# Queueing one engine's share of a second chain behind the first at the seam of two blocks

## The chip, the cores and the metric

The kernel runs on one core of a Trainium2 chip. The core has a matmul engine (TensorE, PE in the rows, with its weight loads as PEld), two vector engines with different abilities (VectorE, DVE; GpSimd, POOL), an activation engine (ScalarE, ACT) and a queue that issues the transfers from memory (SyncE, SP). Each engine works through its own instructions in order and waits on semaphores for the others. The metric is the device time of one launch in microseconds (us).

## The reference, cut to what matters

Two transformer blocks run one after the other on 256 tokens of width 1024, in float32. Block 1 has two layers of mixed attention, each ending in a layer norm. Block 2 is a gated delta-rule mixer (in chunks of 64 tokens, forward and backward), a chunk MLP, and an expert-choice FFN with 16 experts. A second sequence, the context, passes through the same mixer first, only for its final states, which are the latent sequence's initial states:

```python
mod = silu(c) @ w_mod + b_mod                       # sh1 sc1 gt1 sh2 sc2 gt2
c_in = rms_norm(h_ctx, norm1_g) * (1 + csc1) + csh1
qc, kc, vc, gc, bc = gdn_streams(c_in @ w_in, ...)
_, s_f, s_b = gdn_two_dirs(qc, kc, vc, gc, bc, 0, 0)          # context
a_in = rms_norm(h_lat, norm1_g) * (1 + sc1) + sh1             # the rows
ql, kl, vl, gl, bl = gdn_streams(a_in @ w_in, ...)
o_lat, _, _ = gdn_two_dirs(ql, kl, vl, gl, bl, s_f, s_b)      # latent
h_lat = h_lat + gt1 * mix_out(...)
h_lat = h_lat + gt2 * expert_choice_ffn(rms_norm(h_lat, norm2_g) * (1 + sc2) + sh2)
```

Inside `gdn_two_dirs` each chunk needs the inverse of a unit lower triangular 64 x 64 matrix made from the keys: "the solve" below.

## The kernel before, in words

The program is written in one order, and a planner places each engine's instructions in a list ahead of time: at each point of its planned time an engine takes the ready instruction that was written first. So an instruction written later can stand ahead of one written earlier if the earlier one was still waiting in the plan. `issue_after(ins)`, here `self.after(...)`, adds an edge within one engine: of the instructions written in its block, those that run on the engine of `ins` are placed behind `ins`; those on other engines get no edge.

On-chip memory comes from pools of named tiles. With `reuse_waits="tile"` a tile of a later pool waits only for the earlier tiles whose place it takes. `scope` opens the pools of a block; tags in `order` get a pool of their own. PSUM has 8 banks: in block 1 two `mm`, four for two `s` tiles, one `o`, one `g`; in block 2 two `mm`, five `s`, one `g`.

Matmuls of the projections split both operands in a high and a low part (three matmuls for one). `halves` makes a weight's parts: ScalarE copies (L344), VectorE or GpSimd subtracts (L345, by the letters of `self.pat`). `affine_T` makes the activations' parts: for each of 8 slices k of 128 features VectorE computes scale and shift from PSUM (L493), ScalarE the same into the high part (L494), and for odd k VectorE, for even k GpSimd subtracts (L495).

The seam between the blocks, in the order in which it is written:

1. the end of `layer(1)`: output projection (`rows_out`, L476), residual and layer norm of two tiles of 128 rows (up to L755);
2. `hook1(99)`: the modulation column gt1, `gemv` with a 1024 x 1024 weight in four chunks of 1 MB through two `wg` tiles (L366 loads, L372 multiplies, 16 matmuls a chunk), added to the bias in `gacc` (L375), then broadcast (`bcast`). gt2 is computed the same way at step 13 of layer 1;
3. `block2`: `rms_rows` (squares on ScalarE, L1158; five small VectorE operations and two ScalarE ones in `rsqrt`, L410 to L418), scaling to `uv` (L1628), 16 transposes (`trans_all`, L513), and `affine_T`;
4. `ctx_A`: two ScalarE copies of the context's matrices;
5. `gdn_columns` for the latent k: the first of two projections goes through `proj_2` (L444, 48 matmuls), which takes slice after slice as `affine_T` delivers them; the second through `proj_t` (L433 to L435); then a convolution and a gate;
6. `tinv_64(ctx)`: GpSimd clears `E` (L1508), VectorE and ScalarE fill it (L1514, L1516, L1522, L1524), and for each of four combinations four rounds of matmul and VectorE operation follow (L1537, L1541, L1544, L1547; the matmuls are `chunk_dots`, L1316);
7. `gdn_decays`, `lat_A`, `lat_16` for the latent; `gdn_uw(ctx)` (L1396, L1398); then `gdn_scan(ctx)` (L1440 makes `kg` on GpSimd) and the latent's `tinv_64` in turns; and the rest of the latent.

After block 2 the experts' weights stream through 23 slots of 1 MB (`rw`, `w`), loaded ahead as far as there is room.

Of the kernel before, what the change touches and what calls it, by code (L numbers as in the profile page):

```python
# [9 lines left out]
F32 = mybir.dt.float32  # L10
# [5 lines left out]
PSUM = bass.MemoryType.PSUM  # L16
# [3 lines left out]
KT = 8  # L20
DEPTH = 2
ALPHA = (2.0 * DEPTH) ** 0.25
LN_EPS = 1e-5
RMS_EPS = 1e-6
BIG = 2.0 ** 100
# [222 lines left out]
class Kern:  # L248
    def __init__(self, ctx, tc, io, out, dbg=None):
        self.ctx, self.tc, self.nc, self.io, self.out, self.dbg = ctx, tc, tc.nc, io, out, dbg or {}  # L250
        P = lambda name, bufs, **k: ctx.enter_context(tc.tile_pool(name=name, bufs=bufs, **k))
        self.const = P("const", 1)
        self.keep = P("keep", 1)
        self.wp = P("wp", 1)
        self.late = False
        self.sb = self.ps = self.cx = self.last_dma = None
        self.nsplit = 0
        self.c = {}
        self.pat = "VVP"
# [25 lines left out]
    @contextmanager  # L285
    def side(self):

        with (self.tc.tile_pool(name="cx", bufs=1, side="right") as self.cx,
              self.tc.tile_pool(name="cl", bufs=1) as self.cl):
            yield  # L290

    def kt(self, shape, tag):
        return self.keep.tile(shape, F32, name=tag, tag=tag)
# [12 lines left out]
        return self.ps.tile(list(shape), F32, name="o", tag="o", bufs=1)  # L306

    def psg(self, shape=(128, 512)):
        return self.ps.tile(list(shape), F32, name="g", tag="g", bufs=1)

    def wtile(self, n=2048):
        return self.wp.tile([128, 2048], F32, name="w", tag="w", bufs=NW)[:, :n]
# [124 lines left out]
    def proj_2(self, p, w, uT):  # L437

        uh, ul = uT
        hv = [self.halves(w[:, :, 128 * i:128 * i + 128]) for i in range(2)]  # L440
        for k in range(8):
            for i, (wh, wl) in enumerate(hv):
                for a, b, j in ((wh, uh, 0), (wh, ul, 1), (wl, uh, 2)):
                    self.nc.tensor.matmul(p[:, i, :], a[:, k, :], b[:, k, :], start=(k == 0 and i == 0 and j == 0),  # L444
                                          stop=(k == 7 and j == 2), skip_group_check=True)
# [37 lines left out]
        self.lo_engine().tensor_sub(p[:, 1], v, p[:, 0])  # L483
        return p[:, 0], p[:, 1]

    def affine_T(self, src, A, B, tag="uT"):

        nc = self.nc
        uh, ul = (self.t([128, 8, 256], tag, 2, FR) for _ in range(2))
        for k in range(8):  # L490
            s = src(k)
            t = self.t([128, 2 if ("uT" in self.by_tag) else 1, 256], "aff", 2)[:, 0]
            nc.vector.tensor_scalar(t, s, A[:, k:k + 1], B[:, k:k + 1], op0=ALU.mult, op1=ALU.add)  # L493
            nc.scalar.activation(uh[:, k], s, AF.Identity, bias=B[:, k:k + 1], scale=A[:, k:k + 1])  # L494
            (nc.vector if k % 2 else nc.gpsimd).tensor_sub(ul[:, k], t, uh[:, k])  # L495
        return uh, ul

    def trans(self, x, pool=None):
# [446 lines left out]
    def block1(self):  # L945
        nc = self.nc
# [6 lines left out]
        m = {"cols": self.t([128, 2, 8], "ada_cols")}  # L953
# [55 lines left out]
        m2 = {}  # L1009
# [15 lines left out]
        def hook1(i):  # L1025
            if i == 3:
                self.ctx_early(ctx)
            if i == 3:
                n.update(self.ada(1, ("gate",)))
            if i == 99:  # L1030
                self.modulation2(m2, ("gt1",))
            if i == 11:
                self.modulation2(m2, ("sc2", "sh2"))
                self.router(m2)
            if i == 13:
                self.modulation2(m2, ("gt2",))
        self.layer(0, uT, x, m, hook0, first)
        st.close()
        n = m["next"]
# [5 lines left out]
        nc.vector.tensor_mul(B, lc[:, 1], n["scale"])  # L1045
        nc.vector.tensor_add(B, B, n["shift"])
        ps = [self.pst().rearrange("p a (b t) -> p (a b) t", b=2) for _ in range(2)]
        uT = self.affine_T(self.trans_all([x[:, 0], x[:, 1]], ps), A, B)
        ctx = {"pre": "c"}
        self.pat = "P"  # L1050
        self.gdn_columns(ctx, m["ctx"], (("k", 4),))
# [569 lines left out]
    def block2(self, x, m, ctx):  # L1621
# [5 lines left out]
            r = self.rms_rows([x[:, tt]], f"lr{tt}", [y[:, tt]])  # L1627
            nc.vector.tensor_scalar(y[:, tt], x[:, tt], r, None, op0=ALU.mult)  # L1628
        ps = [self.bank().rearrange("p (a b) t -> p a (b t)", a=2) for _ in range(4)]
        uT = self.affine_T(self.trans_all([y[:, 0], y[:, 1]], ps), m["sc1"], m["sh1"])  # L1630
        self.ctx_A(ctx)
        R = {"pre": "l"}
        self.pat = "VP"
        self.gdn_columns(R, uT, (("k", 4),), True)
        self.pat = "VVP"
        for _ in self.tinv_64(ctx):
            pass
        self.gdn_decays(R, uT, "l")
        self.lat_A(R)
        self.lat_16(R)  # L1640
        self.gdn_uw(ctx)
        a, b = self.gdn_scan(ctx), self.tinv_64(R)
        for _ in zip_longest(a, b):
            pass
# [269 lines left out]
    def run(self):  # L1914
        with self.side():
            self.ns = 3
            with self.scope("b1", order=("", "wg")):
                x, m, ctx = self.block1()
            self.ns = 2
            with self.scope("b2", order=B2):  # L1920
                self.block2(x, m, ctx)
        with self.scope("mo"), ExitStack() as st:

            rp = [st.enter_context(self.tc.tile_pool(name=f"ring{j}", bufs=1, side="right", reuse_waits="tile"))
                  for j in range(NR)]
            i = [0]

            def ring():
                j = ORDER[i[0] % len(ORDER)]
                i[0] += 1  # L1930
                return self.wtile() if j < 0 else rp[j].tile([128, 2048], F32, name="rw", tag="rw")
            self.moe(x, m, ring)
# [14 lines left out]
```

## Time and profile before

| | us |
|---|---|
| median of 3 runs | 1303.93 (1303.8 to 1306.29) |
| the profiled execution | 1295.95 |
| its span in the profile | 1294.2 |

| engine | busy us | share of the span |
|---|---|---|
| TensorE | 1048.7 | 81% |
| VectorE | 558.6 | 43% |
| ScalarE | 387.4 | 30% |
| GpSimd | 264.6 | 20% |

A row of a time line has start and duration in us, engine, line, operation, output and inputs with their shapes, and in brackets how long the engine had been idle and what it waited for. The mean of the transfers is 255 GB/s; the experts take the last third of the span. The seam lies near 560 to 606 us.

### The profile page before, as it was taken

What the parts mean: (1) busy time and instruction counts of PE and PEld (TensorE: products, weight loads), DVE (VectorE), ACT (ScalarE), POOL (GpSimd) and SP (SyncE); (2) the same over time, 40 slices, a digit from 0 to 9 for tenths busy, and PEclk for the clock granted to TensorE, in tenths of its full rate; (3) what the DMA queues carried; (4) which work ended last, traced back from release to release, by engine and by line L of the source; (5) the groups of instructions that cost most, each with busy time, mean ns of one, the idle gap of its engine ahead of it and who ended that gap; (6) DMA issues with size and microseconds to landing.
All of it is one profiled execution on the core that took longest, in us unless ns stands there. A gap on an engine that the chain in (4) does not pass through costs nothing.

```text
span 1294.2 us, 22853 instructions
## 1 busy us (share of the span) xinstructions
PE 1048.7 (81%) x9488; PEld 733.4 (57%) x9488; DVE 558.6 (43%) x1315; ACT 387.4 (30%) x899; POOL 264.6 (20%) x235
## 2 busy tenths in 40 slices
PE   5878999986869999957879999898666766676665
PEld 2766787776757876736778888654322432232232
DVE  2585357777696445586585435620100010010002
ACT  2334337635334425525542434310000000000002
POOL 1431132266421221152424343200000000000000
PEclk9899999999989999977979999899877787787777
DMA  8745864434224385521211555979999999999996
GB/s 357 263 160 204 311 228 171 140 130 176 102 88 168 140 305 191 215 78 39 95 58 40 192 202 215 363 288 417 421 420 419 421 419 420 419 420 420 420 421 247
DMA packets 52569, 330.07 MB, mean 255 GB/s; under 512 B 8049, under 2 KB 9969, under 8 KB 14321
## 3 DMA queue, kind: packets, MB, share of 16 engines
q1 hardware_dynamic: 52464, 328.61, 64.9%
q8 instruction: 74, 1.21, 0.4%
q14 instruction: 31, 0.25, 0.1%
HBM read 327.54 MB, written 1.05 MB: 254 GB/s over the span
## 4 chain that ended last, share of the span: by engine, by line
PE 42%; DMA 35%; DVE 11%; POOL 4%; ACT 4%; issue 4%; POOLq 0%; SPq 0%; DVEq 0%; ACTq 0%
DMA rw<-in_w_up 13%; DMA rw<-in_w_down 11%; DMA rw<-in_w_gate 5%; PE mm L433 4%; PE mm L435 4%; PE mm L434 4%; DMA w<-in_w_up 3%; PE s L476 3%; PE mm L457 3%; PE g L372 3%; DMA wg<-in_w_ada 3%; POOL wl L345 2%; PE s L1316 2%; ACT wh L344 2%; PE s L553 2%
## 5 line engine op out<-in xcount | busy, mean ns | idle before, releaser
L433 PE MATMUL mm<-uT,wh 128*128 128x256 f32 x576 | 173.1, 301 | 11.1 <-DVE yT L1247 6.6
L435 PE MATMUL mm<-uT,wl 128*128 128x256 f32 x576 | 167.7, 294 | 15.9 <-DVE wl L345 9.2
L344 ACT CAST wh<-w 128x1024 fp32r<-128x1024 f32 x124 | 127.6, 1033 | 154.1 <-PE mm L434 114.9
L434 PE MATMUL mm<-uT,wh 128*128 128x256 f32 x576 | 167.4, 291 | 0.0
L345 POOL TENSOR_TENSOR wl<-w,wh 128x1024 fp32r<-128x1024 f32 x47 | 114.2, 2431 | 200.3 <-ACT wh L344 168.1
L435 PEld LDWEIGHTS mm<-uT,wl 128*128 128x128 f32 x576 | 111.6, 195 | 25.9 <-DVE wl L345 10.1
L433 PEld LDWEIGHTS mm<-uT,wh 128*128 128x128 f32 x576 | 112.6, 196 | 22.7 <-issue 14.5
L1808 PE MATMUL g<-rw,XE 128*32 128x256 f32 x928 | 84.2, 469 | 41.3 <-DMA rw<-in_w_up 41.3
L345 DVE TENSOR_TENSOR wl<-w,wh 128x1024 fp32r<-128x1024 f32 x77 | 96.6, 1254 | 43.9 <-ACT wh L344 43.5
L434 PEld LDWEIGHTS mm<-uT,wh 128*128 128x128 f32 x576 | 112.4, 195 | 5.2 <-issue 4.0
L1808 PE MATMUL o<-rw,XE 128*32 128x256 f32 x944 | 85.3, 464 | 32.8 <-DMA rw<-in_w_gate 32.8
L1824 DVE TENSOR_TENSOR hd<-hd,g 128x256 f32<-128x256 f32 x16 | 6.7, 419 | 214.4 <-PE g L1808 214.4
L1820 ACT ACTIVATE hd<-o 128x256 f32<-128x256 f32 x16 | 6.1, 384 | 310.9 <-PE o L1808 310.9
L1852 PE MATMUL mm<-rw,hT 128*32 128x256 f32 x880 | 67.9, 446 | 18.7 <-DMA rw<-in_w_down 13.2
L1808 PEld LDWEIGHTS g<-rw,XE 128*32 128x32 f32 x928 | 31.8, 128 | 86.1 <-DMA rw<-in_w_up 66.8
L1808 PEld LDWEIGHTS o<-rw,XE 128*32 128x32 f32 x944 | 31.1, 125 | 76.8 <-DMA rw<-in_w_gate 53.9
L457 PE MATMUL mm<-wh,uT 128*128 128x256 f32 x256 | 54.0, 298 | 3.1 <-ACT wh L344 2.5
L1852 PEld LDWEIGHTS mm<-rw,hT 128*32 128x32 f32 x880 | 27.9, 124 | 49.5 <-DMA rw<-in_w_down 21.7
L457 PEld LDWEIGHTS mm<-wh,uT 128*128 128x128 f32 x256 | 41.6, 194 | 7.1 <-ACT wh L344 2.9
L565 ACT ACTIVATE P<-s,nm 128x256 f32<-128x256 f32 (+1 forms) x88 | 35.8, 419 | 18.9 <-DVE nm L558 18.7
L476 PE MATMUL s<-wh,m 128*128 128x512 f32 x128 | 41.2, 401 | 0.0
L457 PE MATMUL mm<-wl,uT 128*128 128x256 f32 x128 | 37.9, 296 | 0.8 <-DVE wl L345 0.7
(644 smaller groups left out, 1987.9 us busy)
## 6 DMA issues: line engine op xcount, KB each, us to landing
rw<-in_w_gate SPq DMA_DIRECT2D x59, 1024.0 KB, 19.9
rw<-in_w_up SPq DMA_DIRECT2D x58, 1024.0 KB, 19.9
rw<-in_w_down SPq DMA_DIRECT2D x55, 1024.0 KB, 19.8
w<-in_w_in SPq DMA_DIRECT2D x48, 1024.0 KB, 4.7
wg<-in_w_mod SPq DMA_DIRECT2D x24, 1024.0 KB, 4.9
wg<-in_w_ada SPq DMA_DIRECT2D x21, 1024.0 KB, 5.3
w<-in_w_out SPq DMA_DIRECT2D x12, 1024.0 KB, 4.8
w<-in_w_up SPq DMA_DIRECT2D x6, 1024.0 KB, 19.8
```

Of the source, the lines that this page charges most:

```text
L344: self.nc.scalar.copy(hi, w)
L345: self.lo_engine().tensor_sub(lo, w, hi)
L372: nc.tensor.matmul(p[32 * j:32 * j + 32, :], vec[:, 2 * q + kk, :], w[:, kk, 256 * j:256 * j + 256], start=(kk == 0 and (q == 0 or not who ...
L433: mm(out, wh[:, k, :], uh[:, k, :], start=(k == 0), stop=False)
L434: mm(out, wh[:, k, :], ul[:, k, :], start=False, stop=False)
L435: mm(out, wl[:, k, :], uh[:, k, :], start=False, stop=(k == 7))
L457: mm(p[:, tt, :], a[:, k, t], b[:, k % 4, :], start=(k == 0 and tt == 0 and j == 0), stop=(k == 7 and j == 2), skip_group_check=True)
L476: mm(Y(tt, n), a[:, t], b[:, 512 * n:512 * n + 512], start=(k2 == 0 and kk == 0 and i == 0), stop=(k2 == 3 and kk == 1 and i == 2))
L553: nc.tensor.matmul(S[:, h, o:o + n], qT[rows, t], kT[rows, :n], start=False, stop=True, skip_group_check=True)
L565: nc.scalar.activation(Pm[:, h, o:o + n], S[:, h, o:o + n], AF.Exp, bias=nm[:, i:i + 1], scale=0.125, accum_out=l[:, i:i + 1])
L1808: nc.tensor.matmul(pp[32 * j:32 * j + 32, :], XE[:, k, 32 * (e % 4):32 * (e % 4) + 32], w[:, kk, 256 * j:256 * j + 256], start=(k == 0), s ...
L1852: nc.tensor.matmul(py[32 * j:32 * j + 32, :], hT[:, cb, 32 * jj:32 * jj + 32], w[:, kk, 256 * j:256 * j + 256], start=(k == 0), stop=(k == 7))
```

## The change

Seven edits. gt2 is computed after layer 1, behind gt1. The context's `ctx_A` and `tinv_64` are written behind the latent k columns, and these and `gdn_uw(ctx)` behind the last two subtractions of the affine pass (`rows_end`). The affine passes of layer 1 and of block 2, and `proj_2`, take the slices in the order `KO`; two neighbouring slices lie in one bank. The tags `c2v` and `gacc` get pools of their own in block 1, and `g` a bank of its own for both blocks.

```diff
+KO = (0, 2, 1, 3, 4, 6, 5, 7)
...
+        self.rows_end = [None, None]
...
-              self.tc.tile_pool(name="cl", bufs=1) as self.cl):
+              self.tc.tile_pool(name="cl", bufs=1) as self.cl,
+              self.tc.tile_pool(name="psG", bufs=1, space=PSUM, reuse_waits="tile") as self.pg):
             yield
+        self.pg = None
...
-        return self.ps.tile(list(shape), F32, name="g", tag="g", bufs=1)
+        return (self.pg or self.ps).tile(list(shape), F32, name="g", tag="g", bufs=1)
...
-        for k in range(8):
+        for k in KO:
             for i, (wh, wl) in enumerate(hv):
...
-    def affine_T(self, src, A, B, tag="uT"):
+    def affine_T(self, src, A, B, tag="uT", order=range(8)):
...
-        for k in range(8):
+        for k in order:
...
-            (nc.vector if k % 2 else nc.gpsimd).tensor_sub(ul[:, k], t, uh[:, k])
+            sub = (nc.vector if k % 2 else nc.gpsimd).tensor_sub(ul[:, k], t, uh[:, k])
+            self.rows_end = [self.rows_end[1], sub]
...
             if i == 99:
-                self.modulation2(m2, ("gt1",))
+                self.modulation2(m2, ("gt1", "gt2"))
...
-            if i == 13:
-                self.modulation2(m2, ("gt2",))
...
-        uT = self.affine_T(self.trans_all([x[:, 0], x[:, 1]], ps), A, B)
+        uT = self.affine_T(self.trans_all([x[:, 0], x[:, 1]], ps), A, B, order=KO)
...
-        uT = self.affine_T(self.trans_all([y[:, 0], y[:, 1]], ps), m["sc1"], m["sh1"])
-        self.ctx_A(ctx)
+        uT = self.affine_T(self.trans_all([y[:, 0], y[:, 1]], ps), m["sc1"], m["sh1"], order=KO)
+
         R = {"pre": "l"}
+        end = self.rows_end
         self.pat = "VP"
         self.gdn_columns(R, uT, (("k", 4),), True)
         self.pat = "VVP"
-        for _ in self.tinv_64(ctx):
-            pass
+        with self.after(end[0]), self.after(end[1]):
+            self.ctx_A(ctx)
+            for _ in self.tinv_64(ctx):
+                pass
         self.gdn_decays(R, uT, "l")
         self.lat_A(R)
         self.lat_16(R)
-        self.gdn_uw(ctx)
+        with self.after(end[0]), self.after(end[1]):
+            self.gdn_uw(ctx)
...
-            with self.scope("b1", order=("", "wg")):
+            with self.scope("b1", order=("", "c2v", "gacc", "wg")):
```

## Rows read from the trace of the kernel before

**Rows 1.** Stages: busy us of each engine, granted TensorE clock, DMA share, GB/s.

```profile
core 0: us, PE busy (x) PEld busy (x) DVE busy (x) ACT busy (x) POOL busy (x), PEclk, DMA share, GB/s
576.00:592.00 16.00, 3.87 (x18) 3.17 (x18) 14.44 (x26) 9.55 (x15) 7.87 (x7) 0.50 0.01 4
...
606.00:640.00 34.00, 32.29 (x402) 27.92 (x404) 19.11 (x49) 17.27 (x45) 11.28 (x8) 1.00 0.26 94
...
665.00:704.00 39.00, 31.13 (x299) 27.27 (x299) 26.53 (x47) 14.29 (x19) 14.29 (x12) 0.91 0.22 75
```

**Rows 2.** Time line of VectorE in the seam: start us, duration us.

```profile
574.17 2.24 DVE L755 TENSOR_TENSOR x<-x,PT 128x512 f32<-128x512 f32 x2
576.34 2.11 DVE L1514 TENSOR_SCALAR i<-cT,c 128x256 f32<-128x256 f32 x2
...
579.11 0.11 DVE L410 TENSOR_SCALAR lr0qa<-lr0ss 128x1 f32<-128x1 f32 x1
...
585.84 2.37 DVE L418 TENSOR_TENSOR lr1rs<-lr1qr,lr1qb 128x1 f32<-128x1 f32 x1
...
589.27 0.74 DVE L1628 TENSOR_SCALAR uv<-x,lr1rs 128x1024 f32<-128x1024 f32 x1
```

**Rows 3.** Time line of ScalarE: the second tile's squares.

```profile
576.44 1.06 ACT L1158 ACTIVATE uv<-x 128x1024 f32<-128x1024 f32 x1 [1.12 <-DVE x L755]
```

**Rows 4.** Time line of TensorE: last gt1 chunk, first transposes.

```profile
562.68 1.07 PE L372 MATMUL g<-wg,c2v 128*32 128x256 f32 x16
...
586.07 1.94 PE L513 MATMUL s<-c,uv 128*128 128x128 f32 x8 [13.50 <-DVE uv L1628]
```

**Rows 5.** Time line of SyncE: last prefetches, first load after them.

```profile
832.09 3.76 SPq L1846 DMA_DIRECT2D w<-in_w_down  x2
852.30 0.33 SPq L1846 DMA_DIRECT2D rw<-in_w_down  x1
```

**Rows 6.** Time line of GpSimd in the seam.

```profile
563.86 2.48 POOL L1398 TENSOR_TENSOR kb<-yT,cbe 128x512 f32<-128x512 f32 x2 [1.21 <-PE g L372]
...
578.28 1.93 POOL L1508 MEMSET E<- 128x2048 f32 x1
580.18 1.07 POOL L1440 TENSOR_TENSOR kg<-yT,ceg 128x512 f32<-128x512 f32 x1
585.57 2.62 POOL L345 TENSOR_TENSOR wl<-w,wh 128x1024 fp32r<-128x1024 f32 x1 [4.32 <-ACT wh L344]
```

**Rows 7.** Time line of VectorE in the affine pass.

```profile
590.79 0.55 DVE L493 TENSOR_SCALAR aff<-s,m_sc,m_sh 128x256 f32<-128x256 f32 x1 [0.78 <-PE s L513]
...
592.77 0.54 DVE L493 TENSOR_SCALAR aff<-s,m_sc,m_sh 128x256 f32<-128x256 f32 x1 [0.26 <-POOL uT L495]
595.59 0.42 DVE L1537 TENSOR_TENSOR X<-s,c 128x256 f32<-128x256 f32 x1 [2.27 <-PE s L1316]
...
603.51 0.42 DVE L495 TENSOR_TENSOR uT<-aff,uT 128x256 fp32r<-128x256 f32 x1 [0.63 <-ACT uT L494]
```

**Rows 8.** Two matmul groups: count, min/median/max ns, first and last start.

```profile
L444 PE MATMUL mm<-uT,wh x32: 279/384/580, 592.6 to 604.9; 128*128 128x256 f32 x32
...
L1316 PE MATMUL s<-E,A x16: 311/312/366, 592.0 to 595.2; 64*64 64x64 f32 x16
```

**Rows 9.** Chain that ended last, pieces on TensorE: start, us, count.

```profile
487.07 1.01 PE g L372 x16
...
596.96 2.86 PE mm L444 x12
...
600.08 1.63 PE mm L444 x12
```

**Rows 10.** Time line of VectorE: the context's solve and its first reader.

```profile
607.55 0.41 DVE L1547 TENSOR_TENSOR E<-E,s 128x256 f32<-128x256 f32 x1
...
629.86 0.42 DVE L1547 TENSOR_TENSOR E<-E,s 128x256 f32<-128x256 f32 x1 [1.12 <-PE s L1316]
...
647.02 0.68 DVE L1396 TENSOR_TENSOR vb<-s,cbeta 128x512 f32<-128x512 f32 x1
```

**Rows 11.** DMA issues: count, KB each, median us from issue to landing.

```profile
wg<-in_w_mod SPq DMA_DIRECT2D x24, 1024.0 KB, 4.9
```

## What I predict

> **What bounds the kernel now.** I read the table of stages first, then the time line of VectorE in front of block 2, then those of the engines beside it, and last the chain. The table [rows 1] shows TensorE busy for 32.29 of the 34 us from 606 to 640, at full clock: the bulk of block 2 is TensorE's. Just ahead it is not: from 576 to 592 TensorE is busy 3.87 of 16 us with a granted clock of 0.50. VectorE is busy 14.44 of those 16 us. So the seam between the blocks is set by VectorE, and its time line says with what [rows 2]: the last normalised rows of x end at 576.41 (574.17 + 2.24), but then comes L1514, which belongs to the context's solve; the rows' own first small operation starts at 579.11, although ScalarE has the second half's squares at 577.50 [rows 3]. The rows' last scaling (L1628) ends at 590.01. TensorE idles 13.50 us before the first transposes at 586.07 [rows 4].
>
> From there on nothing returns the time. Block 2 is TensorE-bound, and at its end the expert weights are already loaded as far as there is room: the last two prefetches go out at 832.09, the next load only at 852.30, when a slot comes free [rows 5]. The tail starts from full slots, so a block 2 that ends earlier moves all of it.
>
> **The change, part by part.** All sums are made against the profiled execution (1295.95 us, span 1294.2); the median of the runs shown, 1303.93, lies 7.98 above it, and I carry differences over.
>
> *Context behind the rows.* VectorE's part of `ctx_A`, `tinv_64(ctx)` and `gdn_uw(ctx)` may not issue before the last two subtractions of the affine pass. In the order KO the last two are k = 5 and 7, and odd k go to VectorE: both edges end on VectorE, none on GpSimd. So the edges hold VectorE alone; TensorE's solve matmuls follow through their data, ScalarE's copies of A stay, and GpSimd's memsets and `kg` stay where they are, the last `kg` until 581.25 [rows 6].
>
> With VectorE free, the second half needs 577.50 plus some 1.5 us (two short ScalarE operations and five short VectorE ones) plus 0.74 for L1628: 579.8, which is 10.2 us earlier. That is one end. The other end: L418 on one element per partition took 2.37 us [rows 2], from 585.84 to 588.21, and ended just after GpSimd's split L345, which ran from 585.57 to 588.19 [rows 6]: a VectorE operation can sit out a GpSimd one. If `kg` (to 581.25) and then a split of 2.62 are both sat out, L1628 ends at 584.6, 5.4 us earlier. I take `kg` alone, as it is certainly there: 581.25 + 0.74 = 582.0, a gain of 8.0.
> [...]
>
> *The affine pass.* Before, it lasts from 590.79 to 603.93 [rows 7]. VectorE's own work in it is 8 x 0.54 + 4 x 0.42 = 6.0 us. Its first and third L493 start 1.98 apart: k = 0 and 1 share a bank and run one behind the other there, so four pairs alone would take 7.9. The other 5 us are the solve: L1537 at 595.59 came after 2.27 us of waiting for TensorE with the pass queued behind it. With the solve gone and neighbours in different banks I take 7 us; bounds 6.0 and 7.9.
>
> *The first projection.* L444 starts 1.8 us after the first L493, at 592.6, and its last matmul starts at 604.9 [rows 8]; say 605.2 for its end. Its 48 matmuls ran at 2.86/12 = 0.238 us each early and 1.63/12 = 0.136 later [rows 9], the clock having come up some 8 us after the start. So alone they take about 33 x 0.238 + 15 x 0.136 = 9.9 us: from 584.6 to 594.5, and the affine pass (582.8 to 589.8) stays ahead of them. That is 10.7 us earlier. The 48 solve matmuls that stood between them (three groups like the one of 16 in [rows 8]) took the other 2.7 of the 12.6 us and now come later, at full clock: I give back 2. Net -8.7.
>
> *What the delayed solve costs.* Its VectorE work, four L1514, two transposes, four copies, some 8 us as in the seam, now starts at 590 and is hidden by what TensorE has without it, the rest of the k columns and the decays; VectorE is busy 19.11 of 34 us there [rows 1], so there is room. Its next reader is L1396 in `gdn_uw(ctx)`, at 647.02, 17 us after the solve's last L1547 at 629.86 [rows 10]. I cost it at nothing; without that cover it is the first rival.
>
> *gt2 moved to the end of block 1.* Four chunks of 16 matmuls, the first at 487.07, leave a stretch where TensorE is the chain; one takes 1.01 [rows 9], so at most 4.1 us. Its loads (four of 1 MB, four of biases) leave SP's queue there too, and gt1's chunks move up into their slots, so part of the 4.1 is only exchanged. One gt1 chunk already ran in the idle seam at 562.68 [rows 4]; later chunks land there. With one accumulation, VectorE saves three small additions. Bounds 0 and -4.1; I take -2.
>
> *Own places.* `c2v`, `gacc` and the bank of `g` no longer share with block 2. What sharing cost in the seam was a GpSimd `kb` at 563.86 that had waited 1.21 us [rows 6], on an engine that was not awaited: 0, at most -1. KO in layer 1 feeds a projection that takes k in natural order and starts after the pass: 0, within 1 either way.
>
> Sum: -8.7 - 2 = -11 (rounded). 1303.93 - 11 = 1293.
>
> **Rivals.** *The solve becomes the late one (slower).* It is ready to iterate at about 590 + 8 = 598 and makes 16 rounds. Before, it took from 592.0 to 629.86 [rows 8, 10], 2.37 us a round: the end would be 636, just when `gdn_uw(ctx)` wants it after an 11 us shift (647 - 11). Its first four rounds, beside L444, took 4.0 each (to 607.55 plus 0.41): 16 at that pace end at 662, 26 late, and the time is about 1303.93 - 11 + 26 = 1319. It makes the change a loss beyond 0.2% from (650 - 598)/16 = 3.2 us a round. For it: its combinations run one after the other, and VectorE now also has the columns. Against it: the last twelve rounds took 1.9 each once the clock was up. At 3.5 a round the time is 1311. Chance 0.12.
>
> *The gt2 columns stand in front of the transposes (same).* TensorE takes its queue in order; a chunk needs one of two `wg` slots, and a load takes 4.9 us [rows 11]. Two pairs after 563.8 end near 576, hidden. If four loads went one by one, 4 x (4.9 + 1.0) = 23.6 puts the transposes at 587.4: 5.4 of the gain is gone, and with the GpSimd bound of -5.4 for the rows nothing is left: about 1303. For it: the loads were planned against a shorter queue. Against it: TensorE's 13.50 us gap. Chance 0.10.
>
> *Given back later.* From 665 to 704 TensorE is busy only 31.13 of 39 us [rows 1], waiting on short VectorE chains of block 2's own solve. These chains now share VectorE with the context's. If half of the gain goes there: 1299. Chance 0.08.
>
> *More than forecast.* The rows' k columns arrive 11 us earlier, and the context's matmuls, now later, fill those same gaps of up to 8 us: -11 - 7 = -18, 1286. Chance 0.12.
>
> **How the numbers follow.** Forecast (gain 6 to 16, 1288 to 1298) 0.58; more 0.12; given back 0.08; same 0.10; slower 0.12. Within 0.2% (2.6 us), about what a measurement of this kernel can tell from no change: 0.10; faster 0.58 + 0.12 + 0.08 = 0.78; slower 0.12. The low end is the rows' best (10.2 earlier, 10.9 net), the whole 4.1 of gt2, 7 of filled gaps and 1 for the shared places: -23, 1281. The high end, 1303, leaves out the slower case and about half of "same", some 0.17.
>
> **What would show it.** In the changed trace: no L1514 on VectorE between the last L755 and the affine pass; first L513 6 to 10 us closer to that L755 than the 9.66 us now; the affine pass in 6 to 8 us with no L1537 in it; L444 without solve matmuls between; gt2's last chunks in the seam; and the first wait for expert weights 11 us earlier. Wrong if L1628 still ends more than 10 us after the last L755, if L513 waits for L372's loads, or if `gdn_uw(ctx)` waits for the solve.

## The result, and the profile after

The changed kernel takes 1290.37 us in the median of 4 runs (1290.09 to 1293.32); the kernel before, beside it, 1303.87. The ratio is 0.9899, 95% interval 0.9879 to 0.9919: faster, 2.6 us under the forecast of 1293 and inside its range. The profiled execution took 1290.4 us with a span of 1288.6, only 5.6 under the span before, because that execution of the kernel before was itself 8 us under its median. The number came out, but two of its terms did not, as the profile shows stage by stage.

The stages again (answering to [rows 1]; same columns):

```profile
576.00:592.00 16.00, 13.52 (x71) 12.06 (x71) 11.73 (x20) 7.35 (x12) 6.86 (x7) 0.67 0.01 4
606.00:640.00 34.00, 31.12 (x404) 25.92 (x403) 19.57 (x45) 15.22 (x43) 9.23 (x9) 1.00 0.18 63
665.00:704.00 39.00, 34.76 (x286) 30.71 (x285) 20.74 (x38) 14.16 (x19) 12.05 (x11) 0.82 0.23 75
```

TensorE works in the seam now (13.52 of 16 us instead of 3.87). But from 665 to 704 it needs 34.76 busy us at a granted clock of 0.82, where before it was 31.13 at 0.91.

The time line of VectorE in the seam (answering to [rows 2] and [rows 7]):

```profile
566.29 2.25 DVE L761 TENSOR_TENSOR x<-x,PT 128x512 f32<-128x512 f32 x2
...
570.79 1.76 DVE L350 TENSOR_TENSOR wl<-w,wh 128x1024 fp32r<-128x1024 f32 x1 [0.87 <-ACT wh L349]
572.48 0.99 DVE L420 TENSOR_TENSOR lr0qb<-lr0qr 128x1 f32<-128x1 f32 x1
573.39 0.15 DVE L420 TENSOR_TENSOR lr1qb<-lr1qr 128x1 f32<-128x1 f32 x1
...
574.07 1.67 DVE L1632 TENSOR_SCALAR uv<-x,lr0rs 128x1024 f32<-128x1024 f32 x1
575.66 2.89 DVE L1632 TENSOR_SCALAR uv<-x,lr1rs 128x1024 f32<-128x1024 f32 x1
579.34 0.99 DVE L498 TENSOR_SCALAR aff<-s,m_sc,m_sh 128x256 f32<-128x256 f32 x2 [0.79 <-PE s L519]
...
587.17 0.43 DVE L500 TENSOR_TENSOR uT<-aff,uT 128x256 fp32r<-128x256 f32 x1 [0.30 <-ACT uT L499]
587.51 0.61 DVE L1518 TENSOR_SCALAR i<-cT,c 128x256 f32<-128x256 f32 x2
...
591.64 2.72 DVE L1528 COPY E<-i 32x512 f32<-32x512 f32 x1
```

That of GpSimd beside it (answering to [rows 6]):

```profile
571.43 2.02 POOL L1444 TENSOR_TENSOR kg<-yT,ceg 128x512 f32<-128x512 f32 x1
573.39 1.80 POOL L1512 MEMSET E<- 128x2048 f32 x1
575.16 2.84 POOL L350 TENSOR_TENSOR wl<-w,wh 128x1024 fp32r<-128x1024 f32 x1
```

No L1518 stands between the last L761 and the affine pass any more. The rows' last scaling ends at 578.55, 10.0 us behind x (568.54) instead of 13.6, and not the 5.6 forecast: both L1632 are stretched from 0.75 to 1.67 and 2.89 us, and each ends 0.55 us after an instruction of GpSimd, the memset and the split. The pass lasts 8.26 us instead of 13.14 and has no L1541 in it. The solve's first instruction follows the last subtraction at once.

The time line of TensorE: the last two gt2 chunks, the first transposes (answering to [rows 4]), the solve's first matmuls, and the second half of the second k projection:

```profile
563.48 1.93 PE L377 MATMUL g<-wg,c2v 128*32 128x256 f32 x16 [4.74 <-DMA wg<-in_w_mod]
566.36 1.94 PE L377 MATMUL g<-wg,c2v 128*32 128x256 f32 x16 [0.95 <-DMA wg<-in_w_mod]
575.79 1.97 PE L519 MATMUL s<-c,uv 128*128 128x128 f32 x8 [7.50 <-DVE uv L1632]
...
598.01 0.47 PE L1320 MATMUL s<-E,A 64*64 64x64 f32 x2 [2.11 <-ACT E L1526]
...
600.20 0.58 PE L438 MATMUL mm<-uT,wh 128*128 128x256 f32 x1
```

The first projection as a group (answering to [rows 8], same columns):

```profile
L449 PE MATMUL mm<-uT,wh x32: 278/368/582, 580.5 to 589.1; 128*128 128x256 f32 x32
```

The solve's last subtraction and its first reader on VectorE (answering to [rows 10]):

```profile
625.27 0.42 DVE L1551 TENSOR_TENSOR E<-E,s 128x256 f32<-128x256 f32 x1 [0.98 <-PE s L1320]
642.29 0.68 DVE L1400 TENSOR_TENSOR vb<-s,cbeta 128x512 f32<-128x512 f32 x1
```

And the time line of SyncE at the end of block 2 (answering to [rows 5]):

```profile
827.76 3.26 SPq L1854 DMA_DIRECT2D w<-in_w_down  x2
846.70 0.33 SPq L1854 DMA_DIRECT2D rw<-in_w_down  x1
```

The first load that waits for a slot goes out 5.6 us earlier (852.30 before), just what the span has lost: the tail only follows. So the first projection ends 15.7 us earlier than before (589.5 to 605.2), 7.9 of them because x ended earlier, yet at the end of block 2 only 5.6 are left.

To see where they go I cut every profiled execution at the same instructions: layer 1 is from the start of its last transpose of x (L513 in the kernel before) to the start of the last L755, x's last normalised rows; the seam from there to the start of the last L444 matmul; block 2 from there to the router's last matmul (L1733). The ratios are those of the timed runs:

```
kernel            layer 1   seam  block 2   seam + block 2   ratio (95%)
before             287.4    29.3   232.5        261.8        1
before_again       284.3    29.0   230.8        259.8        1.0001 (0.9974 to 1.0028)
edges_only         289.4    20.4   243.4        263.8        0.9979 (0.9959 to 0.9998)
gt2_only           279.7    28.8   235.9        264.7        0.9941 (0.9914 to 0.9969)
gt2_ctxA           282.1    31.7   234.2        265.9        0.9942 (0.9914 to 0.9970)
gt2_KO_aff         284.2    30.7   233.9        264.6        0.9941 (0.9916 to 0.9967)
gt2_KO             279.0    27.9   227.3        255.2        0.9860 (0.9815 to 0.9905)
gt2_KO_places      281.4    28.5   226.6        255.1        0.9884 (0.9851 to 0.9917)
after_no_edges     282.5    28.7   226.7        255.4        0.9857 (0.9833 to 0.9881)
after_uv_edge      280.7    26.5   227.0        253.5        0.9856 (0.9819 to 0.9893)
after              279.1    21.3   243.5        264.8        0.9899 (0.9879 to 0.9919)
after_again        277.8    21.4   243.7        265.1        0.9904 (0.9883 to 0.9924)
after_pe_held      281.4    21.3   243.5        264.8        0.9904 (0.9880 to 0.9928)
after_cols_held    281.0    21.1   247.3        268.4        0.9989 (0.9961 to 1.0018)
```

A stretch comes from one execution and scatters by some 3 us; the ratios carry the verdicts.

### The profile page after: what moved, and what is told of

It reads as the page before. It is cut to its first block, busy times and chain, and to the rows that moved or that the text cites. A ratio compares the mean times of both kernels' runs of the same rounds, so it can differ in the third digit from the quotient of the medians.

```text
span 1288.6 us, 22845 instructions
## 1 busy us (share of the span) xinstructions
PE 1045.7 (81%) x9488; PEld 737.1 (57%) x9488; DVE 551.8 (43%) x1312; ACT 385.6 (30%) x899; POOL 267.1 (21%) x235
## 4 chain that ended last, share of the span: by engine, by line
PE 41%; DMA 35%; DVE 10%; ACT 6%; POOL 5%; issue 3%; SPq 0%; POOLq 0%; DVEq 0%; ACTq 0%
DMA rw<-in_w_up 15%; DMA rw<-in_w_down 11%; DMA rw<-in_w_gate 5%; PE mm L438 4%; PE mm L440 4%; PE mm L439 4%; PE mm L462 3%; DMA wg<-in_w_ada 3%; PE s L481 3%; POOL wl L350 3%; PE g L377 2%; PE s L1320 2%; ACT wh L349 2%; PE o L588 2%; PE s L559 1%
## 5 line engine op out<-in xcount | busy, mean ns | idle before, releaser
L350 POOL TENSOR_TENSOR wl<-w,wh 128x1024 fp32r<-128x1024 f32 x47 | 114.5, 2439 | 192.2 <-ACT wh L349 154.5
L438 PEld LDWEIGHTS mm<-uT,wh 128*128 128x128 f32 x576 | 113.8, 198 | 17.0 <-issue 7.3
L350 DVE TENSOR_TENSOR wl<-w,wh 128x1024 fp32r<-128x1024 f32 x77 | 97.0, 1261 | 53.3 <-ACT wh L349 52.9
L439 PEld LDWEIGHTS mm<-uT,wh 128*128 128x128 f32 x576 | 114.1, 198 | 5.6 <-issue 4.8
L1816 PE MATMUL o<-rw,XE 128*32 128x256 f32 x944 | 88.3, 480 | 33.8 <-DMA rw<-in_w_gate 33.8
L1860 PE MATMUL mm<-rw,hT 128*32 128x256 f32 x880 | 64.5, 429 | 24.0 <-DMA rw<-in_w_down 18.6
```

Of the source, the lines that this page charges most:

```text
L350: self.lo_engine().tensor_sub(lo, w, hi)
L438: mm(out, wh[:, k, :], uh[:, k, :], start=(k == 0), stop=False)
L439: mm(out, wh[:, k, :], ul[:, k, :], start=False, stop=False)
L1816: nc.tensor.matmul(pp[32 * j:32 * j + 32, :], XE[:, k, 32 * (e % 4):32 * (e % 4) + 32], w[:, kk, 256 * j:256 * j + 256], start=(k == 0), s ...
L1860: nc.tensor.matmul(py[32 * j:32 * j + 32, :], hT[:, cb, 32 * jj:32 * jj + 32], w[:, kk, 256 * j:256 * j + 256], start=(k == 0), stop=(k == 7))
```

## The experiments

Before them I held this theory: the edges gain in the seam and give it back in block 2, and gt2 carries more than its 2 us. The rival was the forecast's own account.

**before_again**: the kernel before, unchanged, for the scatter.

> The kernel before, unchanged, profiled a second time. The profiled execution of before took 1295.95 us where its runs have a median of 1303.87; that of the changed kernel took 1290.4, as its runs do. If the first profile was an ordinary execution, this one takes 1296 again and the ratio is 1.000. If it was an unusually fast one, this one takes about 1303, and the place where its extra 8 us lie (the seam, block 2, or the stream of expert weights) says which rows of the first profile can be compared with the changed kernel's.

Measured: 1302.68 us, 1292.61 to 1310.03 over 12 runs. A single time of this kernel means little; medians and intervals do.

**edges_only**: the edges alone, on the kernel before. Its last subtraction on VectorE is that of k = 7.

```diff
+            self.rows_end[k % 2] = sub
...
-        self.ctx_A(ctx)
...
-        for _ in self.tinv_64(ctx):
-            pass
+        with self.after(end[1]):
+            self.ctx_A(ctx)
+            for _ in self.tinv_64(ctx):
+                pass
...
-        self.gdn_uw(ctx)
+        with self.after(end[1]):
+            self.gdn_uw(ctx)
```

> Before, with the context's solve written behind the latent k columns and VectorE's share of it held behind the last subtraction of the affine pass; gt2, KO and the shared places as before. The forecast (the seam sets the time and nothing returns it): 9 us faster. The rival (the gain of the seam is given back in block 2, because the solve's first matmuls now stand in TensorE's queue ahead of the second half of the k columns and wait for VectorE and ScalarE): 0 to 4 us faster, with idle TensorE between the first k column and the second.

Measured: 1299.64 us, ratio 0.9979. The seam gains 8.9 us and block 2 returns 10.9; by the timed runs 2.7 us are left.

**gt2_only**: gt2 moved, nothing else.

```diff
-                self.modulation2(m2, ("gt1",))
+                self.modulation2(m2, ("gt1", "gt2"))
...
-            if i == 13:
-                self.modulation2(m2, ("gt2",))
```

> Before, with gt2 computed after layer 1 behind gt1, all else as before. The forecast: 2 us faster (0 to 4). The rival (most of the change's gain is made before the seam, since the last rows of x were ready 7.9 us earlier in the changed kernel's profile): 6 to 9 us faster.

Measured: 1292.85 us, ratio 0.9941, which is 7.7 us of 1302.

**after_no_edges**: the changed kernel with its order of writing, but without the two `with self.after(...)`.

```diff
-        with self.after(end[0]), self.after(end[1]):
-            self.ctx_A(ctx)
-            for _ in self.tinv_64(ctx):
-                pass
+        self.ctx_A(ctx)
+        for _ in self.tinv_64(ctx):
+            pass
...
-        with self.after(end[0]), self.after(end[1]):
-            self.gdn_uw(ctx)
+        self.gdn_uw(ctx)
```

> The changed kernel without the edges: the context's solve is still written behind the latent k columns, but nothing holds it. The forecast: the 9 us of the seam are gone, 1299 to 1301. The rival that the edges gain little: within 3 us of the changed kernel, 1288 to 1293. A third reading (the edges cost time, since they delay the solve): faster than 1288.

Measured: 1283.82 us, ratio 0.9857, better than the changed kernel. The edges cost time here, though alone, on the kernel before, they cost none (edges_only). Two questions follow: why, and what gains 0.8% beyond gt2.

**after_again**: the changed kernel on the chip of the next three.

> The changed kernel itself, beside the others on one chip. Theory (the edges are worth less than nothing: what they win in front of the first projection comes back in block 2, and gt2 and the rest carry the gain): ratio 0.987 to 0.992 to the kernel before, and from the last matmul of the first projection to the router some 10 us more than without the edges. Rival (the edges gain, and the kernel without them was only favoured by its executions): 0.984 or lower, that is at or under the 0.9857 measured without the edges.

Measured: 1288.24 us, ratio 0.9904, as the theory has it; from the first projection to the router it takes 17 us more than without the edges (243.7 and 226.7), not some 10.

**after_pe_held**: the solve held on TensorE too, so that its first matmuls can't stand ahead of the second half of the second k projection (600.20 above).

```diff
-            mm(out, wl[:, k, :], uh[:, k, :], start=False, stop=(k == 7))
+            self.cols_end = mm(out, wl[:, k, :], uh[:, k, :], start=False, stop=(k == 7))
...
-        with self.after(end[0]), self.after(end[1]):
+        with self.after(end[0]), self.after(end[1]), self.after(self.cols_end):
             self.ctx_A(ctx)
```

> The changed kernel with the context's solve also held on TensorE, behind the last matmul of the latent k columns. In the changed kernel 16 of the solve's matmuls stood in TensorE's list ahead of the second half of the second k projection, from 595.5 to 600.2, with 4 us of waiting for the solve's E. Theory (this place in the list is what gives the seam's gain back): the second half of the second projection starts 4 to 5 us earlier relative to the first projection's end, lat_A too, and the time falls by 3 to 8 us, ratio 0.982 to 0.987. Rival (the late solve itself is the price, wherever it stands in the list; it now starts still later): no better than the changed kernel, 0.988 to 0.995.

Measured: 1289.05 us, ratio 0.9904. The theory is wrong: with the solve's matmuls out of the way the half waits just as long, as TensorE's time line shows:

```profile
598.91 0.55 PE L439 MATMUL mm<-uT,wh 128*128 128x256 f32 x1 [3.79 <-ACT sg L664]
```

**gt2_KO_places** and **gt2_ctxA**: which of the other edits carries the 0.8%. The first adds KO and the own places to gt2_only, as in the change; the second only the place of the two copies:

```diff
-        self.ctx_A(ctx)
         R = {"pre": "l"}
...
+        self.ctx_A(ctx)
         for _ in self.tinv_64(ctx):
```

> The kernel before with gt2 moved, the order KO and the own places, without the edges and with the two copies of the context's A where they were. gt2 alone gave 0.9941, the whole change without edges 0.9857. Theory (KO and the own places carry the other 0.8%, mostly in block 2): 0.984 to 0.988. Rival (the place of the two copies carries it, as the stretch from the latent's solve to the router is 8 us shorter in all three kernels that have them behind the columns): 0.992 to 0.996.

> The kernel before with gt2 moved and the two copies of the context's A written behind the latent k columns; no KO, no own places, no edges. Theory (KO and the own places carry what is left): 0.992 to 0.996, as with gt2 alone. Rival (the place of the copies carries it): 0.984 to 0.988, with the last scan subtraction some 60 us instead of 68 us after the last vb of the latent.

Measured: 1284.53 us, ratio 0.9884, and 1293.28 us, 0.9942. The first lies a little above the theory's range. The copies' place is worth nothing; KO or the places are worth it, and the gain lies in block 2.

**after_cols_held**: VectorE's share of the solve held back further, behind the last convolution of the k columns (`conv`, kept in `cols_end`).

```diff
-        with self.after(end[0]), self.after(end[1]):
+        with self.after(self.cols_end[0]):
             self.ctx_A(ctx)
```

> The changed kernel with VectorE's part of the context's solve held further back, behind the last convolution of the latent k columns instead of behind the affine pass. In the changed kernel the solve's E (L1518, L1520, L1528) stands between these convolutions, and from the first projection's last matmul to lat_A it takes 51.3 us, against 38.8 in every kernel without the edges. Theory A (what the delayed solve costs is that its E sits in VectorE's queue among the k columns): that stretch falls to 45 us or less, TensorE's 4 us of waiting ahead of the second half of the second projection is gone, and the time falls to 1280 to 1286, ratio 0.983 to 0.988. Theory B (the solve is wanted as early as it can be had, wherever it stands; its delay comes out later): the stretch shrinks, but what follows it grows from 192 us, and the ratio is 0.990 to 0.998.

Measured: 1298.09 us, ratio 0.9989. Theory A falls: the stretch to lat_A grew from 51.3 to 59.8 us. The ratio is theory B's and a little over, but its picture fails too, as the stretch did not shrink. The time lines show why. First VectorE, the ends of the solve's last two combinations:

```profile
630.69 0.42 DVE L1552 TENSOR_TENSOR E<-E,s 128x256 f32<-128x256 f32 x1 [0.79 <-PE s L1321]
634.78 0.42 DVE L1552 TENSOR_TENSOR E<-E,s 128x256 f32<-128x256 f32 x1 [0.78 <-PE s L1321]
```

Then TensorE, where the solve's last rounds run with waits and nothing between them, and the columns only behind:

```profile
631.64 0.68 PE L1321 MATMUL s<-E,X 64*64 64x64 f32 x16 [0.53 <-DVE X L1542]
632.84 0.68 PE L1321 MATMUL s<-X 64*64 64x64 f32 x16 [0.52 <-DVE X L1546]
634.05 0.68 PE L1321 MATMUL s<-X,E 64*64 64x64 f32 x16 [0.52 <-DVE E L1549]
637.27 0.36 PE L439 MATMUL mm<-uT,wh 128*128 128x256 f32 x1 [1.51 <-DVE yT L1252]
```

**after_uv_edge**: one edge, behind the rows' last scaling; the solve's E may be built in the gaps of the affine pass.

```diff
-            nc.vector.tensor_scalar(y[:, tt], x[:, tt], r, None, op0=ALU.mult)
+            uv_end = nc.vector.tensor_scalar(y[:, tt], x[:, tt], r, None, op0=ALU.mult)
...
-        with self.after(end[0]), self.after(end[1]):
+        with self.after(uv_end):
             self.ctx_A(ctx)
...
-        with self.after(end[0]), self.after(end[1]):
-            self.gdn_uw(ctx)
+        self.gdn_uw(ctx)
```

> The changed kernel with one edge only, for VectorE, behind the rows' last scaling (L1632) instead of behind the affine pass, and none for the context's vb. The solve's E may then be built in the affine pass's gaps, some 9 us earlier than in the changed kernel. Theory A (the rows' chain gains by the edge, the solve's late start costs): the rows' transposes stay 7 to 8 us behind x's end (15 without edges), the stretch from the first projection to the router comes down from 243.5 to 230 to 236, and the time is 1278 to 1284, under the 0.9857 measured without edges. Theory B (whatever is held back in the seam comes back in block 2): 243 us there again and a ratio of 0.987 to 0.992.

Measured: 1282.63 us, ratio 0.9856. The rows' transposes start 7.25 us behind x's end, as theory A has it (14.75 without edges), and block 2 is back at 227.0, so not everything held back returns; but the time is that without edges, not under it. The solve ends early again, on VectorE:

```profile
618.72 0.41 DVE L1551 TENSOR_TENSOR E<-E,s 128x256 f32<-128x256 f32 x1
```

**gt2_KO**: gt2_only with the three uses of KO and no own places.

> The kernel before with gt2 moved and the order KO alone, no own places. With gt2 alone the ratio was 0.9941, with gt2, KO and the own places 0.9884, and the gain lay between the first projection and the router, 235.9 to 226.6 us. Theory (KO gives it): 0.986 to 0.990 and 227 us. Rival (the own places give it): 0.992 to 0.996 and 233 to 236 us.

Measured: 1283.22 us, ratio 0.9860. KO carries it, in kernels without the edges. TensorE runs the 2096 matmuls from the transposes to the router in the same order as in gt2_KO_places, so I put the places at nothing. But how can the order of eight slices gain 8 us 70 us further on? Against gt2_only, the order of those matmuls differs almost to the end: only the last 474 are the same.

**gt2_KO_aff**: KO in block 2's affine pass alone. The pass alternates between banks, but TensorE's order in block 2 differs from that of gt2_only only within the first 378 matmuls from the transposes on.

```diff
-        for k in KO:
+        for k in range(8):
             for i, (wh, wl) in enumerate(hv):
...
-ps), A, B, order=KO)
+ps), A, B)
```

> gt2 moved, and the order KO only in block 2's affine pass; layer 1's pass and the first projection take their slices in the natural order. The pass alternates between banks as with the whole KO, but TensorE's list in block 2 is, from some 50 matmul groups into the projections on, the same as with gt2 alone, while with the whole KO it differs in 286 lines. Theory (KO gains because the list of block 2 comes out in another order, not by its banks): 0.992 to 0.996 as with gt2 alone, the first projection to the router again 233 to 237 us, and TensorE's wait of 6.6 us for the convolution's yT some 70 us behind the first projection is back. Rival (alternating banks gain it): 0.984 to 0.989 and 226 to 229 us.

Measured: 1293.15 us, ratio 0.9941, as with gt2 alone. TensorE's longest waits from 640 to 700 us (who waited for whom, us in total, times, longest), with gt2 alone:

```profile
PE mm L433 <- DVE yT L1245: 6.6, 1, 6.6
```

With the whole KO:

```profile
PE mm L437 <- POOL wl L347: 1.9, 1, 1.9
PE mm L435 <- DVE yT L1247: 1.4, 1, 1.4
```

With KO in the pass alone:

```profile
PE mm L435 <- DVE yT L1247: 7.0, 1, 7.0
```

The same wait, for a convolution in a column of the latent, is 6.6, 1.4 and 7.0 us. It is the list that gains, not the banks.

The wait alone does not carry the gain. Up to the latent's last vb the whole KO gains 2.3 us; the other 7.1 come later, from there to the router (116.6 us with gt2 alone, 109.5 with the whole KO, 116.7 with KO in the pass alone). The matmuls of the chunk MLP's first projection (`proj_n`, 96 of them, some 0.12 us apart) show why. Behind that vb stand, with gt2 alone:

```profile
L457 PE MATMUL mm<-wh,uT x43: 281/283/362, 720.2 to 728.6; 128*128 128x256 f32 x43
L457 PE MATMUL mm<-wl,uT x22: 280/283/385, 720.0 to 728.5; 128*128 128x256 f32 x22
```

With the whole KO:

```profile
L459 PE MATMUL mm<-wh,uT x4: 278/280/366, 719.3 to 719.9; 128*128 128x256 f32 x4
L459 PE MATMUL mm<-wl,uT x2: 280/281/282, 719.5 to 719.8; 128*128 128x256 f32 x2
```

Of these 65 the other 59 now run ahead of that vb. With the edges they do so too, without KO: 7 are left behind it in edges_only.

## Why the prediction was right in number and wrong in two terms

**What the delayed solve costs.** "I cost it at nothing" failed, and with it "From there on nothing returns the time." The forecast looked for the solve's reader: L1396, 17 us behind it. That slack is still there, 16.6 us between 625.69 and 642.29 in the rows above. It is not the reader that is late, but what stands behind the solve in the in-order lists of TensorE and VectorE. From the traces, in us after the start of the last row of x; then the time from the latent's last vb to the router, and how many matmuls of `proj_n` start behind that vb:

```
kernel            solve's last   lat_A's last   latent's   vb to    `proj_n`      ratio
                  subtraction    matmul         last vb    router   behind it
before               54.6           68.1         145.1     116.7          65           1
gt2_only             54.0           67.6         148.1     116.6          65           0.9941
gt2_KO_aff           54.7           68.3         147.9     116.7          65           0.9941
edges_only           56.5           71.4         156.3     107.5           7           0.9979
after_uv_edge        51.9           65.9         145.1     108.5           6           0.9856
gt2_KO               52.8           66.8         145.8     109.5           6           0.9860
after_no_edges       53.6           67.5         146.7     108.7           6           0.9857
after                57.8           72.7         157.4     107.4           7           0.9899
after_pe_held        58.3           72.7         157.3     107.5           7           0.9904
after_cols_held      68.0           80.9         160.7     107.7           8           0.9989
```

lat_A comes 13 to 15 us after the solve in all of them, and it begins the latent's own solve. Among the last six, which have KO in full, the solve's end moves by some 5 us from the first three to the next two and by 10 more to the last, and the time by about 5 and 11 (0.4% and 0.9% of 1302). TensorE's idle time from the first projection to lat_A grows with it, from 1.9 us (gt2_KO, after_no_edges) to 8.3 (the changed kernel) and 12.8 (after_cols_held). after_uv_edge and after_cols_held move VectorE's hold to the one side (freeing the context's vb too) and to the other, and the time followed both. So it is shown that the held solve delays lat_A and that this is not free. The price is not shown apart from the list: each hold also makes another list, and gt2_only has the solve nearly as early as gt2_KO (54.0 and 52.8) but is 0.8% slower. The solve's rounds are a chain of short waits; I read the seam, where TensorE idles anyway, as cheap cover for them.

This was the first rival, "the solve becomes the late one", though not by its measure: the rounds took (625.69 - 600.31)/16 = 1.6 us each, not the 3.2 from which it was to decide. A part stays open. Beyond lat_A the kernels with the edges lose another 5 us up to the latent's last vb (84.5 to 84.9 us in four traces, against 79.0 to 80.2 in gt2_KO, gt2_KO_places, after_no_edges and after_uv_edge), but after_cols_held does not (79.8). In the changed kernel TensorE works there mostly at a granted clock of 0.50 (from 654.8 to 668.4 and from 675.2 to 685.5), with two waits of 3.75 and 3.62 us, from 651.5 and from 672.1. The stretches of the changed kernel from 79 us behind x (columns as in [rows 1]):

```profile
647.00:657.00 10.00, 4.83 (x55) 4.20 (x55) 9.93 (x18) 4.12 (x8) 4.98 (x3) 0.89 0.00 0
657.00:667.00 10.00, 10.00 (x69) 9.19 (x68) 8.38 (x28) 3.05 (x7) 2.12 (x2) 0.50 0.01 2
667.00:677.00 10.00, 5.76 (x39) 5.29 (x39) 6.47 (x12) 6.29 (x8) 0.00 (x0) 0.84 0.35 117
677.00:687.00 10.00, 10.00 (x67) 8.51 (x68) 3.54 (x7) 3.27 (x5) 3.26 (x3) 0.58 0.24 69
```

The same of after_no_edges:

```profile
652.00:662.00 10.00, 6.52 (x80) 5.61 (x80) 9.35 (x23) 6.15 (x12) 5.53 (x4) 0.93 0.24 96
662.00:672.00 10.00, 8.37 (x40) 7.90 (x41) 8.22 (x18) 4.83 (x6) 1.22 (x2) 0.56 0.14 49
672.00:682.00 10.00, 8.94 (x97) 7.56 (x97) 7.41 (x13) 4.74 (x8) 4.02 (x4) 1.00 0.41 137
682.00:692.00 10.00, 10.00 (x109) 8.76 (x110) 3.86 (x8) 0.00 (x0) 3.88 (x4) 1.00 0.01 2
```

Each of the two gaps is paid twice here, as idle time (3.75 and 3.62 us) and in the granted clock of the work behind it (0.50 and 0.58 in the rows); after_no_edges has one such stretch (0.56), the changed kernel two. Whether the late solve or the accident of the list makes the second, no run separates.

**The seam.** For the projection's end the forecast had -10.7, and the seam gave -8.0 (29.3 to 21.3). The term that failed is the rows' scaling: 3.6 us earlier behind x, not 8.0. Some 3 of the missing 4.4 us are the two L1632 (1.67 and 2.89 us instead of 0.75), which sat out GpSimd, the split as well as the memset; VectorE's own split of a weight (L350, 1.76 us from 570.79) stood in front of them. The bound of 5.4 was the nearer, and in edges_only, where two of the short operations took 0.99 and 2.19 us instead of 0.15 (L417 at 584.13, L419 at 585.23) and the two scalings 0.76 and 0.75, it is nearly met: the last scaling ends 8.4 us behind x, 5.2 earlier. The projection took back 1.5 of it: it starts 1.2 us behind the first L498 instead of 1.8 and takes 9.0 instead of 9.9, as the granted clock rose from 0.50 to 1.00 some 6 us after its start (at 586.4) and not the forecast's 8 (7.1 in the trace of before, at 599.7). The affine pass was put at 7 us, at most 7.9; it takes 8.26, which did not count, as the projection keeps pace with it. So the forecast's own signs were met in part only: the first transposes start 7.25 us behind x, 2.4 closer than 9.66 and not 6 to 10; the last scaling ends 10.0 us behind x, on the border named for "wrong"; and the first wait for expert weights came 5.6 us earlier, not 11.

**gt2.** The direction was right, the size was not: forecast -2 with a bound of -4.1, measured -7.7 (gt2_only). Layer 1 is 277.8 to 284.2 us, mean 280.8, in the eleven traces with gt2 moved, and 284.3 to 289.4, mean 287.0, in the three without: -6.2. TensorE's busy time in it is the same on average, 249.8 and 249.9 us; its idle time fell from 37.2 to 31.0. So the chunks went where TensorE had idled, as the forecast had it, but the gain is more than their 4.1, and what the rest is was not told apart. From x to the router the trace of gt2_only is not shorter than the two of the kernel before (264.7 us against 261.8 and 259.8), so the traces bear out the timed 7.7 in part only. The last two chunks landed in the idle time ahead of the last rows of x, waiting for their loads (4.74 and 0.95), with no transposes held up: "The gt2 columns stand in front of the transposes" did not happen, as the L519 waited for L1632 alone. That rival's 1303 was also too high by its own rows: its two bounds set the same moment, so the later one decides, and transposes at 587.4 leave a gain of 3.3 beside gt2's 2, which is 1299.

**KO.** "0, within 1 either way" was said of layer 1, where KO changes nothing that counts (279.0 us with gt2_KO, 279.8 with gt2_only). In block 2 it gained 8 to 10 us in the kernels without edges, by a way that the forecast did not have: the planner's list, which puts 59 more matmuls of `proj_n` ahead of the latent's last vb. In the changed kernel it gains nothing more. The edges alone already put them there (edges_only in the table), and TensorE's order in block 2 is matmul for matmul the same in edges_only and in the changed kernel. **Own places**: 0, as forecast.

So the gain of the changed kernel is in the main that of gt2 and of the edges: -7.7 (gt2_only) and -2.7 (edges_only), -10.4 together, which agrees with the measured -13 within the intervals (no run has the two together without KO). The forecast had -2 and -8.7: two errors that cancel, so the number is luck. The edges' -2.7 is itself a balance. They bring 9 us in the seam, yet the latent's last vb comes 11 us later behind x (145.1 to 156.3), and 9 come back behind it with `proj_n` (116.7 to 107.5); in the traces that leaves 2 us lost, within their scatter. Where KO has already moved `proj_n`, the later vb remains (145.8 to 157.4), with 2 us back (109.5 to 107.4), and the timed price is 5 us. "More than forecast", with gaps of TensorE filled, was nearest to what the kernel without edges does (1283.82), but it is the chunk MLP's projection that moves ahead, not the context's matmuls.

## What to carry to other kernels

A chain that isn't awaited by its reader can still be awaited by its queue: ask what stands behind it on each in-order engine before its delay is called free. Give a hold its narrowest place: beside KO it cost nothing behind the rows' scaling, 5 us behind the affine pass, 17 behind the columns. What an edit is worth depends on the list that it meets: the same edges gained 2.7 us on the kernel before. Where a planner writes the lists, an edit of no weight can move the time by more than the one under test, so compare the lists and time each edit alone.

## What the runs showed of the hardware

Beside an instruction of GpSimd some VectorE operations took longer and others did not. In the changed kernel the first L1632 took 1.67 us from 574.07, instead of 0.75, and ended 0.55 us after the memset that ran from 573.39 to 575.19; beside the same memset the operations on one element per partition took 0.15 to 0.16 each (L420 to L423, from 573.39 on). Beside `kg`, which ended at 573.45, the other L420 took 0.99 from 572.48, to that instruction's end. L1528, 0.57 to 0.58 us in its later instances, took 2.72 at 591.64, beside GpSimd's split of 2.43 us from 591.46, with a convolution of the latent k columns behind it. What decides which operation takes longer, no run tells apart.

Two executions of the same list differ from the start. The first 50 us of the kernel before:

```profile
0.00:50.00 50.00, 32.28 (x216) 19.45 (x217) 15.70 (x48) 12.88 (x23) 8.72 (x23) 0.93 0.82 326
```

The same of before_again:

```profile
0.00:50.00 50.00, 31.11 (x213) 18.81 (x214) 15.19 (x46) 12.69 (x22) 8.74 (x23) 0.74 0.82 320
```

The granted clock was 0.93 and 0.74 there, and layer 1 begins 8.4 us later in the second. A scatter of that size, as large as most of the edits here, lets one execution's rows give differences and not a time: the one that the forecast was worked out from lay 8 us under the median.
